# Hybrid decoder layer on one core: inputs of the dense products first on ACT and DVE, and a third buffer for their outputs

## The chip, the core and the metric

The kernel runs on one core of one Trainium2 chip. The metric is the device time of one execution in microseconds (us), as the median of several runs. A core has five engines with instruction queues of their own, each worked off in order: TensorE (PE, with its weight loads as PEld), VectorE (DVE), ScalarE (ACT), GpSimd (POOL) and SyncE (SP), which here issues all the DMAs.

## The reference

One layer on x (1024 x 1024, float32) with conditioning c. Cut to what matters:

```python
mod = c_act @ ada_w[l] + ada_b[l]
shift1, scale1, gate1, shift2, scale2, gate2 = [m[:, None, :] for m in jnp.split(mod, 6, axis=-1)]
h = x * (1.0 + scale1) + shift1
z = h @ w_in[l]                                   # 1024 x 3984
z_h, z_g, z_r = jnp.split(z, [N_HGRN_COLS, N_HGRN_COLS + N_GLA_COLS], axis=-1)
o_h = hgrn2_mixer(z_h, lower_bounds[l], hgrn_norm_g[l])
o_g = gla_mixer(z_g, gla_alpha_up[l], gla_alpha_b[l], gla_norm_g[l])
o_r = rwkv7_mixer(z_r, rwkv_mu[l], rwkv_w0[l], ...)
o = jnp.concatenate([o_h, o_g, o_r], axis=-1) @ w_out[l]
x = layer_norm(DEEPNORM_ALPHA * x + (1.0 + gate1) * o, ln1_g[l], ln1_b[l])
h = x * (1.0 + scale2) + shift2
m = jnp.square(jax.nn.relu(h @ mlp_w_up[l])) @ mlp_w_down[l]   # inner width 4096
x = layer_norm(DEEPNORM_ALPHA * x + (1.0 + gate2) * m, ln2_g[l], ln2_b[l])
```

The three mixers are recurrences over the sequence. All 16 heads carry a state from one chunk to the next, so the mixers of one piece of the sequence follow those of the piece before.

## The kernel before

The sequence is cut into two blocks of 512 positions, and each block into four tiles of 128 for the mixers. Three kinds of work stand in the program.

**Dense products.** The input projection (`z_block`, `z_rest`, `z_last`, here z(0) and z(1) for the two blocks), the output projection with its layer norm (`out_block`) and the MLP (`mlp_chunk`, `mlp_last`). They are computed in split single precision: each operand is a rounded part and a rest, and `mm3` (lines 1328 to 1330) runs three matmuls for each product. `split` makes the two parts: ACT rounds (`wh`, `ah`, line 1278) and DVE takes the rest (`wl`, `al`, line 1279; line 1276 with a scale). A slab of weights is 128 x 512, comes by DMA into a ring `raw` of 5 buffers, and has rings of 4 for `wh` and `wl`; moving operands have rings of 12, `ah` and `al`. Results lie in PSUM tiles `dn` (`tn` late in the program). They are taken out into a ring of 512-wide tiles tagged `s2`, which the profile shows as `s`: z goes out through them (ACT line 1373 or DVE line 1375; for the RWKV columns ACT line 1217 and DVE line 1218) and from there by DMA (lines 1377, 1379) to arrays in device memory, zr, zgc, zgt, zhc and zht; the relu of the MLP is there too (line 1499, then lines 1502 to 1504), and the modulated input of the MLP (`moving`, lines 1298 and 1300, after PE transposes in line 1293). `s2` has 2 buffers.

**Mixers.** `mixers` (line 336) runs over the tiles of a block as a software pipeline: signals, decays, attention by levels (`la_attn`, with DVE lines 417 to 423 and PE line 434), the triangular inverse of the RWKV part (`rw_base`, a DVE loop in lines 701 and 703 on tiles `btw` and `btm` of 48 partitions), and its chain (`rw_chain`). Their tiles come from pools of their own (`mp`, `psm`). They read z from device memory and write their outputs (lines 538 and 825) to an array oD, from which `out_block` reads (line 1305). mix(0) and mix(1) are the mixers of the two blocks, la_end (line 532) is the end of the attention part of a tile.

**Modulation.** `ada_first` and `ada_later` multiply and sum on DVE (line 1244), with weights in tiles `xt`.

**The order.** The class `Order` lays down, while the program is built, in which order each engine's instructions stand. It plays the program through with a cost for every instruction. Each instruction has a rank, made of a level (`level`, called in `build`) and its place in the program; an engine that is free takes the ready instruction of lowest rank whose tiles have room (`pick`, line 1059). mix(0) and mix(1)'s first tiles have level 0, z(1) has level 2, the MLP level 3 and more. So on ACT and DVE the mixers go ahead of z(1) and the MLP wherever both are ready. PE has a rule more: when few dense columns lie in the recent past (`behind`, line 1045), it takes a dense product first.

```python
            if e == PE and behind():
                for x in sorted(ready[e]):
                    if dense[x[1]] and fits(x[1]):
                        return take(x)
```

z(1) and mix(0) stand beside each other; then out_block(0), with z_last(1), the last part of z(1), beside its layer norm; then `mlp_moving`, and mix(1) beside the MLP of block 0, whose rest and the MLP of block 1 run alone.

Of the kernel before, what the change touches and what calls it, by code (L numbers as in the profile page):

```python
# [10 lines left out]
F32 = mybir.dt.float32  # L11
# [8 lines left out]
P = 128  # L20
# [99 lines left out]
class Kern:  # L120
# [83 lines left out]
    def setup_mixers(self, masks, wau, alpha_up, g_up, nrm):  # L204
# [7 lines left out]
        col = self.col  # L212
        self.wau = self.cp.tile([P, 384], F32, name="wau")
        self.load(self.wau, wau)
        self.aup = self.cp.tile([16, 384], F32, name="aup")
        self.load(self.aup, alpha_up)
        self.gup = self.cp.tile([P, 384], F32, name="gup")
        self.load(self.gup, g_up)
# [459 lines left out]
    def rw_base(self, s):  # L678
        nc = self.nc

        blk = self.dr.tile([4, 64, 3, 64], F32, tag="blk", bufs=2, name=self.nm("blk"))
        inv = self.inv[self.ninv % 2]
        self.ninv += 1
        step = 16 * 192 + 16
        for ca in range(4):
            c, a = divmod(ca, 2)
            nc.sync.dma_start(blk[ca], s["E"][c][64 * a:64 * a + 64, a, :, 0:64])
        TW = self.mt([48, 16, 2, 16], "btw")
        X, W = TW[:, :, 0, :], TW[:, :, 1, :]
        for g in range(12):  # L690
            ca, p = divmod(g, 3)
            src = blk[ca, :, p, :].rearrange("(m i) (n j) -> m i n j", i=16, j=16)
            nc.sync.dma_start(X[4 * g:4 * g + 4], self.diag(src))
        nc.vector.memset(W, 0.0)
        nc.vector.memset(TW.rearrange("p s x t -> p (s x t)")[:, 16:512:33], 1.0)
        tmp = self.mt([48, 64], "btm")
        eng = nc.vector
        for t in range(15, 0, -1):
            n = 16 - t
            tv = tmp[:, 0:t * n].rearrange("p (s j) -> p s j", j=n)  # L700
            eng.tensor_tensor(tv, X[:, 0:t, t:t + 1].broadcast_to([48, t, n]),
                              W[:, t:t + 1, t:16].broadcast_to([48, t, n]), ALU.mult)
            eng.tensor_tensor(W[:, 0:t, t:16], W[:, 0:t, t:16], tv, ALU.add)
        nc.scalar.copy(X, W.rearrange("p s t -> p t s"))
        for g in range(12):
            ca, p = divmod(g, 3)
            c, a = divmod(ca, 2)
            dst = inv[c, 64 * a:64 * a + 64, :, p, :].rearrange("(m i) x (n j) -> m (i x) n j", i=16, j=16)
            nc.sync.dma_start(self.diag(dst), TW[4 * g:4 * g + 4].rearrange("m i x j -> m (i x) j"))
        s["TW"] = self.mt([P, 2, 2, 3, 64], "TW")  # L710
        nc.sync.dma_start(s["TW"].rearrange("s c x p t -> s c (x p t)"), inv.rearrange("c s x p t -> s c (x p t)"))

# [127 lines left out]
F32_WEIGHT, T_WEIGHT = 1.3, 3  # L840

KEEP = 1.2

SWITCH, ISSUE = 130, 20
DMA_ISSUE, DMA_START, DMA_END = 500, 600, 900
# [28 lines left out]
class Order:  # L874
# [141 lines left out]
    def run(self):  # L1016
# [24 lines left out]
        recent, self.sum = collections.deque(), 0  # L1041
        dense = [self.eng[k] == PE and self.ins[k].ins[0].bass_ap.dtype == F32R for k in range(n)]


        def behind():
            while recent and recent[0][0] < t - HAM_TICK:
# [12 lines left out]
        def pick(e):  # L1059
            held = []  # L1060

            def take(x):
                ready[e].remove(x)
                heapq.heapify(ready[e])
                return x[1]

            if e == PE and run:
                x = self.rank[run[0]]
                if x not in ready[e]:
                    return None  # L1070
                run.pop(0)
                return take(x)
# [94 lines left out]
class Full(Kern):  # L1167
# [121 lines left out]
    def moving(self, parts, scale=None, shift=None, late=False, aside=False):  # L1289
        nc = self.nc  # L1290
        ps = self.tps() if late else self.dps()
        for j in range(TPB):
            nc.tensor.transpose(ps[:, j * P:(j + 1) * P], parts[j], self.ident)  # L1293
        if shift is None:
            return self.split(ps, "a", AB, late=late, scale=scale)
        h = self.dt([P, 512], "s2", 2)
        if aside:
            nc.scalar.activation(h, ps, AF.Identity, scale=scale, bias=shift)
        else:
            nc.vector.tensor_scalar(h, ps, scale, shift, ALU.mult, ALU.add)  # L1300
        return self.split(h, "a", AB, late=late)
# [7 lines left out]
    def x_moving(self, b, k, aside=False):  # L1309
        nc = self.nc  # L1310
        x = self.dt([P, 512], "raw", RB)
        h = x if b else self.dt([P, 512], "s2", 2)
        nc.sync.dma_start(x, self.A["xt"][k * P:(k + 1) * P, b * NT:(b + 1) * NT])
        scale, shift = self.mod[:, 8 + k:9 + k], self.mod[:, k:k + 1]
        if aside:
# [45 lines left out]
    def z_block(self, b):  # L1361
# [3 lines left out]

        def put(dst, rows, cols, n):
            def f(m, ps):
                t = self.dt([P, 512], "s2", 2)
                self.flip ^= 1
                if dst is self.zr[b]:  # L1370
                    self.shift(b, rows // P + m, t, ps)
# [93 lines left out]
    def out_block(self, b, late, lv=None):  # L1465
# [5 lines left out]
        for hf in range(2):  # L1471
            cs = slice(hf * 512, (hf + 1) * 512)
            gr = self.row(2, cs, late)

            def ev(t, ps):
                r = self.dt([P, 512], "raw", LR, late=True) if late else self.dt([P, 512], "s2", 2)
                nc.sync.dma_start(r, x[b * NT + t * P:b * NT + (t + 1) * P, cs])
                nc.vector.tensor_tensor(ys[t][:, cs], ps, gr, ALU.mult)
                nc.vector.scalar_tensor_tensor(ys[t][:, cs], r, ALPHA, ys[t][:, cs], ALU.mult, ALU.add)
            self.prod_t(self.A["w_out"][0][:, cs], o, ev, self.tps if late else None)  # L1480
# [12 lines left out]
    def mlp_up(self, fc, h, late):  # L1493
# [1 line left out]
        us = []  # L1495

        def evu(m, ps):
            r = self.dt([P, 512], "s2", 2)
            nc.scalar.activation(r, ps, AF.Relu)  # L1499
            hi = self.dt([P, 512], "ah", AB, F32R, late)  # L1500
            lo = self.dt([P, 512], "al", AB, F32R, late)
# [42 lines left out]
    def mlp_last(self, b, h, acc):  # L1544
# [13 lines left out]
                self.residual(b, acc, gate[:, cs], cs, t)  # L1558

        def add(t, hf, ps):  # L1560
            y = self.dt([P, 512], "s2", 2)
            cs = halves[hf]
            nc.vector.tensor_tensor(y, ps, gate[:, cs], ALU.mult)
            nc.vector.tensor_tensor(acc[t][:, cs], acc[t][:, cs], y, ALU.add)
# [116 lines left out]
```

## Time and profile before

| | before |
|---|---|
| median of 3 runs | 1505.16 us (1505.06 to 1505.33) |
| the profiled execution: its own time | 1511.53 us |
| the profiled execution: its span | 1509.7 us |
| PE busy | 1416.9 us, 94% of the span |
| PEld (weight loads) busy | 1131.9 us, 75% |
| DVE busy | 1052.7 us, 70% |
| ACT busy | 708.0 us, 47% |
| POOL busy | 25.4 us, 2% |
| mean granted clock of TensorE | 0.975 |

The span runs from the first to the last instruction. [...] "Waits" give the idle time of an engine ahead of an instruction and what ended it. Windows count us from the start of the span.

### The profile page before, as it was taken

To read this page: it belongs to the slowest core of one execution; us is meant where nothing else is said; L and a number is where in the kernel's file an instruction comes from. 1 tells how busy PE (TensorE), PEld (TensorE's weight loads), DVE (VectorE), ACT (ScalarE), POOL (GpSimd) and SP (SyncE) were. 2 spreads that over 40 slices of the span, in tenths; PEclk is the share of its full clock that TensorE was granted. 3 is DMA by queue.
4 is the path that set the end of the run, shared out by engine and by line. 5 is a ranking of instruction groups with operands and counts; after the bars stand their busy time and mean duration, and the time that the engine had idled before them with its cause. 6 is when DMAs were issued, how large, how long until landed. Compare 5 with 4: busy or idle time off the path is not lost.

```text
span 1509.7 us, 29223 instructions
## 1 busy us (share of the span) xinstructions
PE 1416.9 (94%) x11226; PEld 1131.9 (75%) x11226; DVE 1052.7 (70%) x2130; ACT 708.0 (47%) x1527; POOL 25.4 (2%) x32
## 2 busy tenths in 40 slices
PE   6999998889899896989899999999999999999996
PEld 5878876667787675767677788787887888888884
DVE  8787479889785576979788765475569445445478
ACT  3543365677756544666657443323343323333331
POOL 1000000000000000000000000000000000000004
PEclk9999999999989997999999999999999999999998
DMA  9998662524424655142423243454336432333331
GB/s 349 331 340 290 191 191 68 164 80 142 125 86 131 197 171 190 51 133 69 122 80 89 67 153 94 143 182 155 91 93 217 144 96 93 97 93 97 94 116 56
DMA packets 163291, 214.00 MB, mean 142 GB/s; under 512 B 39856, under 2 KB 90192, under 8 KB 163152
## 3 DMA queue, kind: packets, MB, share of 16 engines
q1 hardware_dynamic: 163152, 212.14, 44.6%
q8 instruction: 88, 1.44, 0.4%
q14 instruction: 51, 0.42, 0.1%
HBM read 180.03 MB, written 32.06 MB: 140 GB/s over the span
## 4 chain that ended last, share of the span: by engine, by line
PE 47%; DVE 7%; ACT 3%; DMA 2%; issue 1%; POOL 1%; SPq 0%; DVEq 0%; ACTq 0%; POOLq 0%
PE dn L1330 10%; PE dn L1328 10%; PE dn L1329 10%; PE tn L1330 5%; PE tn L1329 5%; PE tn L1328 5%; DMA lnr<-in_ln_b_dram 1%; DVE wl L1279 1%; DMA G<-zgt 1%; PE ml L434 0%; ACT L154 0%; DVE Rs L423 0%; DVE xt L1462 0%; DVE ld L459 0%; PE tn L1293 0%
## 5 line engine op out<-in xcount | busy, mean ns | idle before, releaser
L1278 ACT CAST wh<-raw 128x512 fp32r<-128x512 f32 (+2 forms) x424 | 253.0, 599 | 538.2 <-PE dn L1330 253.3
L1279 DVE TENSOR_TENSOR wl<-raw,wh 128x512 fp32r<-128x512 f32 (+2 forms) x424 | 278.3, 661 | 303.1 <-ACT wh L1278 279.5
L1328 PE MATMUL dn<-wh,ah 128*128 128x512 f32 (+1 forms) x736 | 288.3, 395 | 10.1 <-ACT s L1373 3.4
L1329 PE MATMUL dn<-wl,ah 128*128 128x512 f32 (+1 forms) x736 | 289.9, 394 | 4.6 <-DVE wl L1279 4.6
L1330 PE MATMUL dn<-wh,al 128*128 128x512 f32 (+1 forms) x736 | 287.8, 396 | 4.5 <-DVE al L1504 4.5
L1328 PE MATMUL dn<-ah,wh 128*128 128x512 f32 x560 | 226.7, 406 | 18.6 <-ACT ah L1321 11.4
L1329 PE MATMUL dn<-al,wh 128*128 128x512 f32 x560 | 225.8, 403 | 0.0
L1330 PE MATMUL dn<-ah,wl 128*128 128x512 f32 x560 | 223.5, 402 | 0.9 <-DVE wl L1279 0.7
L1328 PEld LDWEIGHTS dn<-wh,ah 128*128 128x128 f32 x736 | 141.6, 193 | 42.2 <-ACT s L1499 5.2
L1330 PEld LDWEIGHTS dn<-wh,al 128*128 128x128 f32 x736 | 141.6, 193 | 33.2 <-DVE al L1504 6.6
L1329 PEld LDWEIGHTS dn<-wl,ah 128*128 128x128 f32 x736 | 142.3, 193 | 31.3 <-DVE wl L1279 5.3
L1328 PEld LDWEIGHTS dn<-ah,wh 128*128 128x128 f32 x560 | 106.5, 190 | 45.2 <-ACT ah L1321 11.4
L1330 PEld LDWEIGHTS dn<-ah,wl 128*128 128x128 f32 x560 | 105.7, 189 | 24.4 <-DVE wl L1279 2.0
L1329 PEld LDWEIGHTS dn<-al,wh 128*128 128x128 f32 x560 | 106.3, 190 | 22.5 <-issue 0.9
L1330 PE MATMUL tn<-ah,wl 128*128 128x512 f32 x256 | 100.8, 394 | 0.0
L1329 PE MATMUL tn<-al,wh 128*128 128x512 f32 x256 | 100.2, 391 | 0.0
L1328 PE MATMUL tn<-ah,wh 128*128 128x512 f32 x256 | 99.6, 389 | 0.0
L157 ACT ACTIVATE ld<-ld 128x320 f32<-128x320 f32 (+1 forms) x120 | 54.8, 489 | 25.7 <-DVE ld L417 17.5
L1519 DVE TENSOR_TENSOR xt<-xt,dn 128x512 f32<-128x512 f32 x104 | 64.4, 679 | 0.1
L1244 DVE SCALAR_TENSOR_TENSOR xt<-xt,xt 128x1024 f32<-128x1024 f32 x48 | 58.3, 1216 | 8.3 <-DMA xt<-in_ada_wt_dram 8.0
L1329 PEld LDWEIGHTS tn<-al,wh 128*128 128x128 f32 x256 | 48.1, 188 | 11.2
L1328 PEld LDWEIGHTS tn<-ah,wh 128*128 128x128 f32 x256 | 48.1, 188 | 10.6
(288 smaller groups left out, 1960.5 us busy)
## 6 DMA issues: line engine op xcount, KB each, us to landing
raw<-in_mlp_w_up_dram SPq DMA_DIRECT2D x128, 256.0 KB
raw<-in_mlp_w_down_dram SPq DMA_DIRECT2D x128, 256.0 KB
xt<-in_ada_wt_dram SPq DMA_DIRECT2D x48, 512.0 KB
raw<-in_w_in_dram SPq DMA_DIRECT2D x64, 256.0 KB
raw<-in_w_in_dram SPq DMA_DIRECT2D x48, 192.0 KB
raw<-in_w_out_dram SPq DMA_DIRECT2D x32, 256.0 KB
raw<-in_w_in_dram SPq DMA_DIRECT2D x32, 196.0 KB
raw<-in_xt_dram SPq DMA_DIRECT2D x24, 256.0 KB
```

Source lines behind the costliest of these rows:

```text
L157: ins = nc.scalar.activation(out, in_, func, **kw)
L1244: nc.vector.scalar_tensor_tensor(w, w, 1.0, self.cact, ALU.mult, ALU.mult, accum_out=self.sums[:, q:q + 1])
L1278: nc.scalar.copy(hi[:, 0:n], src)
L1279: (eng or nc.vector).tensor_tensor(lo[:, 0:n], src, hi[:, 0:n].bitcast(F32), ALU.subtract)
L1328: nc.tensor.matmul(ps, lh, rh, start=first, stop=False)
L1329: nc.tensor.matmul(ps, lh, rl, start=False, stop=False)
L1330: nc.tensor.matmul(ps, ll, rh, start=False, stop=last)
L1519: nc.vector.tensor_tensor(acc[t][:, cs], acc[t][:, cs], ps, ALU.add)
```

## The change

Three edits. `Order.pick` gets a rule for ACT and DVE: an instruction that uses a tile of the dense products' pools (`dp`, `psd`, `tp`, `pst`) is taken ahead of any other that is ready, whatever its rank, if its tiles have room. The ring `s2` has 3 buffers in place of 2, at each of its uses. And the RWKV inverse's tile `btw` (48 partitions) no longer comes from the mixers' pool: it shares one array `ab` with the small weight `aup` (16 partitions), `btw` at partitions 64 to 111 and `aup` at 0 to 15; `btm` moves to partitions 64 to 111 too.

```diff
--- before.py
+++ after.py
@@ -212,7 +212,9 @@
         col = self.col
         self.wau = self.cp.tile([P, 384], F32, name="wau")
         self.load(self.wau, wau)
-        self.aup = self.cp.tile([16, 384], F32, name="aup")
+
+        self.ab = self.cp.tile([P, 512], F32, name="ab")
+        self.aup = self.ab[0:16, 0:384]
         self.load(self.aup, alpha_up)
         self.gup = self.cp.tile([P, 384], F32, name="gup")
         self.load(self.gup, g_up)
@@ -685,7 +687,7 @@
         for ca in range(4):
             c, a = divmod(ca, 2)
             nc.sync.dma_start(blk[ca], s["E"][c][64 * a:64 * a + 64, a, :, 0:64])
-        TW = self.mt([48, 16, 2, 16], "btw")
+        TW = self.ab[64:112].rearrange("p (i x j) -> p i x j", i=16, x=2)
         X, W = TW[:, :, 0, :], TW[:, :, 1, :]
         for g in range(12):
             ca, p = divmod(g, 3)
@@ -693,7 +695,7 @@
             nc.sync.dma_start(X[4 * g:4 * g + 4], self.diag(src))
         nc.vector.memset(W, 0.0)
         nc.vector.memset(TW.rearrange("p s x t -> p (s x t)")[:, 16:512:33], 1.0)
-        tmp = self.mt([48, 64], "btm")
+        tmp = self.mt([P, 64], "btm")[64:112]
         eng = nc.vector
         for t in range(15, 0, -1):
             n = 16 - t
@@ -841,6 +843,8 @@
 
 KEEP = 1.2
 
+DENSE = ("dp", "psd", "tp", "pst")
+
 SWITCH, ISSUE = 130, 20
 DMA_ISSUE, DMA_START, DMA_END = 500, 600, 900
 
@@ -1041,6 +1045,9 @@
         recent, self.sum = collections.deque(), 0
         dense = [self.eng[k] == PE and self.ins[k].ins[0].bass_ap.dtype == F32R for k in range(n)]
 
+        feeds = [self.eng[k] in (ACT, DVE) and any(t.split("_")[-2] in DENSE for t, _ in self.uses[k])
+                 for k in range(n)]
+
 
         def behind():
             while recent and recent[0][0] < t - HAM_TICK:
@@ -1064,6 +1071,10 @@
                 heapq.heapify(ready[e])
                 return x[1]
 
+            if e in (ACT, DVE):
+                for x in sorted(ready[e]):
+                    if feeds[x[1]] and fits(x[1]):
+                        return take(x)
             if e == PE and run:
                 x = self.rank[run[0]]
                 if x not in ready[e]:
@@ -1293,7 +1304,7 @@
             nc.tensor.transpose(ps[:, j * P:(j + 1) * P], parts[j], self.ident)
         if shift is None:
             return self.split(ps, "a", AB, late=late, scale=scale)
-        h = self.dt([P, 512], "s2", 2)
+        h = self.dt([P, 512], "s2", 3)
         if aside:
             nc.scalar.activation(h, ps, AF.Identity, scale=scale, bias=shift)
         else:
@@ -1309,7 +1320,7 @@
     def x_moving(self, b, k, aside=False):
         nc = self.nc
         x = self.dt([P, 512], "raw", RB)
-        h = x if b else self.dt([P, 512], "s2", 2)
+        h = x if b else self.dt([P, 512], "s2", 3)
         nc.sync.dma_start(x, self.A["xt"][k * P:(k + 1) * P, b * NT:(b + 1) * NT])
         scale, shift = self.mod[:, 8 + k:9 + k], self.mod[:, k:k + 1]
         if aside:
@@ -1365,7 +1376,7 @@
 
         def put(dst, rows, cols, n):
             def f(m, ps):
-                t = self.dt([P, 512], "s2", 2)
+                t = self.dt([P, 512], "s2", 3)
                 self.flip ^= 1
                 if dst is self.zr[b]:
                     self.shift(b, rows // P + m, t, ps)
@@ -1473,7 +1484,7 @@
             gr = self.row(2, cs, late)
 
             def ev(t, ps):
-                r = self.dt([P, 512], "raw", LR, late=True) if late else self.dt([P, 512], "s2", 2)
+                r = self.dt([P, 512], "raw", LR, late=True) if late else self.dt([P, 512], "s2", 3)
                 nc.sync.dma_start(r, x[b * NT + t * P:b * NT + (t + 1) * P, cs])
                 nc.vector.tensor_tensor(ys[t][:, cs], ps, gr, ALU.mult)
                 nc.vector.scalar_tensor_tensor(ys[t][:, cs], r, ALPHA, ys[t][:, cs], ALU.mult, ALU.add)
@@ -1495,7 +1506,7 @@
         us = []
 
         def evu(m, ps):
-            r = self.dt([P, 512], "s2", 2)
+            r = self.dt([P, 512], "s2", 3)
             nc.scalar.activation(r, ps, AF.Relu)
             hi = self.dt([P, 512], "ah", AB, F32R, late)
             lo = self.dt([P, 512], "al", AB, F32R, late)
@@ -1558,7 +1569,7 @@
                 self.residual(b, acc, gate[:, cs], cs, t)
 
         def add(t, hf, ps):
-            y = self.dt([P, 512], "s2", 2)
+            y = self.dt([P, 512], "s2", 3)
             cs = halves[hf]
             nc.vector.tensor_tensor(y, ps, gate[:, cs], ALU.mult)
             nc.vector.tensor_tensor(acc[t][:, cs], acc[t][:, cs], y, ALU.add)
```

In the changed file the lines of the mixers have numbers 2 higher, and those of the dense products 11 higher. The set of instructions is the same; all that moves is their order, up to some 2800 of the 5168 dense matmuls and transposes, and a few at the program's very end.

DVE at the second tile of mix(0), where the RWKV inverse and the attention levels meet (`wl` is a dense weight slab's rest; `TW`, `btw`, `ab`, `btm` belong to the inverse, `ld` and `b` to the attention). Before:

```order
L1279 TENSOR_TENSOR wl_5339<-raw_5336,wh_5338 128x384
L739 COPY_PREDICATED TW_2094<-masks,mr_2864 32x2x3x16 x2
L743 COPY TW_2094<-mr_2864 16x2x3x16 x2
L417 TENSOR_TENSOR ld_3174<-b_2702 128x640
L417 TENSOR_TENSOR ld_3203<-b_2702 128x640
L758 COPY TW_2094<-mr_2934 32x2x3x32
L694 MEMSET btw_2802 48x16x16
L758 COPY TW_2094<-mr_2934 32x2x3x32
L695 MEMSET btw_2802 48x16
L701 TENSOR_TENSOR btm_2817<-btw_2802 48x15
L703 TENSOR_TENSOR btw_2802<-btw_2802,btm_2817 48x15
```

With the change, from the same place:

```order
L1290 TENSOR_TENSOR wl_5443<-raw_5440,wh_5442 128x384
L741 COPY_PREDICATED TW_2092<-masks,mr_2861 32x2x3x16 x2
L745 COPY TW_2092<-mr_2861 16x2x3x16 x2
L419 TENSOR_TENSOR ld_3171<-b_2700 128x640
L419 TENSOR_TENSOR ld_3200<-b_2700 128x640
L760 COPY TW_2092<-mr_2931 32x2x3x32 x2
L696 MEMSET ab 48x16x16
L423 TENSOR_TENSOR ld_3171<-ld_3171,K_2676 128x20x16
L1290 TENSOR_TENSOR wl_5458<-raw_5455,wh_5457 128x384
```

Before, the `wl` at the head is the last for 30 rows; now the next comes after eight.

PE where mix(0) ends and out_block(0) begins (`dn<-consts,raw` is the transposes of oD, `dn<-ah,wh` and its like are products of z(1), `mr` and `ml` belong to mixers). Before:

```order
L1328 MATMUL dn_5951<-ah_5018,wh_6082 128x512
L1293 MATMUL dn_6112<-consts,raw_6110 128x128 x4
L1329 MATMUL dn_5951<-al_5019,wh_6082 128x512
L1330 MATMUL dn_5951<-ah_5018,wl_6083 128x512
L1328 MATMUL dn_5952<-ah_5018,wh_6082 128x512
L1329 MATMUL dn_5952<-al_5019,wh_6082 128x512
L1330 MATMUL dn_5952<-ah_5018,wl_6083 128x512
L1328 MATMUL dn_5953<-ah_5018,wh_6082 128x512
L1329 MATMUL dn_5953<-al_5019,wh_6082 128x512
L1330 MATMUL dn_5953<-ah_5018,wl_6083 128x512
L1293 MATMUL dn_6123<-consts,raw_6121 128x128 x4
```

With the change:

```order
L1341 MATMUL dn_5949<-ah_5014,wl_6079 128x512
L499 MATMUL ml_4705<-V_4177,ld_4689 64x64 x10
L1275 MATMUL ml_4747<-consts,mod 8x128
L1275 MATMUL ml_4827<-consts,mod 8x128
L390 MATMUL ml_7175<-consts,al_7140 16x128
L296 MATMUL mr_6901<-zm_6884,wau 128x128
L298 MATMUL mr_6900<-wk_6895,wau 128x128
L296 MATMUL mr_6901<-zm_6884,wau 128x128
L298 MATMUL mr_6900<-wk_6895,wau 128x128
L296 MATMUL mr_6901<-zm_6884,wau 128x128
L298 MATMUL mr_6900<-wk_6895,wau 128x128
L1304 MATMUL dn_6108<-consts,raw_6106 128x128 x4
```

Before, products of z(1) stand up to and among the transposes, and the last state update of mix(0) (line 497) has 124 of them behind it; now that update (line 499) and mixer work of mix(1) alone stand between the last product of z(1) and the transposes.

ACT at the end of z_last(1), ahead of the MLP's modulated input (line 1373 takes results out to `s`, line 1298 makes the input). Before:

```order
L1373 COPY s_1252_6788<-dn_6584 128x512
L1373 COPY s_1253_6791<-dn_6585 128x512
L1278 CAST wh_10030<-raw_10028 128x512
L1373 COPY s_1254_6794<-dn_6586 128x512
L1373 COPY s_1255_6797<-dn_6587 128x512
L1298 ACTIVATE s_1261_6816<-dn_6811,mod 128x512
L1278 CAST ah_6807<-s_1257_6805 128x512
```

With the change:

```order
L1384 COPY s_1248_6784<-dn_6580 128x512
L1384 COPY s_1249_6787<-dn_6581 128x512
L1384 COPY s_1250_6790<-dn_6582 128x512
L1289 CAST wh_10022<-raw_10020 128x512
L1384 COPY s_1251_6793<-dn_6583 128x512
L621 COPY bs_7060<-mr_7047 128x6
L1309 ACTIVATE s_1257_6812<-dn_6807,mod 128x512
L1289 CAST ah_6803<-s_1253_6801 128x512
```

Before, two results are taken out before a cast of weights and two behind it; now three stand in a row, and mixer work (`bs`) stands between the fourth and the input.

## Rows read from the trace of the kernel before

**Rows 1.** The query on the core: span, and mean granted clock of TensorE.

```profile
core 0: 1509.7 us, clock 0.975
```

**Rows 2.** Windows by stage: us, busy (instructions) by engine, PE clock, DMA share, GB/s.

```profile
100.00:150.00 50.00, 45.93 (x290) 40.70 (x289) 39.47 (x99) 21.33 (x55) 0.00 (x0) 0.93 0.90 292
150.00:210.00 60.00, 58.67 (x268) 48.47 (x267) 33.01 (x64) 23.13 (x44) 0.00 (x0) 1.00 0.63 196
210.00:497.00 287.00, 266.25 (x3691) 206.59 (x3689) 229.15 (x558) 189.99 (x484) 0.00 (x0) 0.96 0.39 117
497.00:605.00 108.00, 90.27 (x381) 71.39 (x380) 69.47 (x132) 51.19 (x93) 1.86 (x2) 0.88 0.60 190
605.00:890.00 285.00, 266.15 (x3588) 204.22 (x3588) 238.68 (x541) 177.80 (x435) 0.00 (x0) 0.98 0.29 85
890.00:950.00 60.00, 60.00 (x265) 49.23 (x264) 29.61 (x48) 18.96 (x32) 0.00 (x0) 1.00 0.47 143
950.00:1470.00 520.00, 516.16 (x2267) 419.46 (x2266) 302.78 (x484) 171.53 (x285) 3.44 (x4) 1.00 0.40 123
```

**Rows 3.** Waits of PE in 210:497: us in total, times, longest.

```profile
PE dn L1328 <- DVE s L1218: 4.5, 4, 2.5
...
PE dn L1328 <- ACT s L1373: 1.4, 1, 1.4
```

**Rows 4.** Waits of PE in 605:890.

```profile
PE dn L1328 <- ACT s L1499: 2.1, 2, 1.3
...
PE dn L1330 <- DVE al L1504: 1.7, 3, 1.3
...
PE dn L1328 <- DVE xt L1517: 1.0, 1, 1.0
```

**Rows 5.** Waits of PE in 100:210.

```profile
PE dn L1328 <- ACT s L1373: 3.4, 2, 1.9
PE dn L1328 <- DVE s L1375: 1.1, 1, 1.1
```

**Rows 6.** Timeline at the second seam: start us, us, engine, line, operation, [idle before <-releaser].

```profile
585.27 1.40 SPq L1377 DMA_DIRECT2D zht<-s  x2
...
588.23 1.22 ACT L1373 COPY s<-dn 128x512 f32<-128x512 f32 x2 [0.50 <-DMA zht<-s]
...
588.87 0.42 SPq L318 DMA_DIRECT2D V<-zht  x1
...
590.76 0.49 SPq L327 DMA_DIRECT2D G<-zht  x1
...
594.10 0.81 DVE L1300 TENSOR_SCALAR s<-dn,mod 128x512 f32<-128x512 f32 x1 [5.64 <-DMA G<-zht]
...
594.65 0.78 ACT L1298 ACTIVATE s<-dn,mod 128x512 f32<-128x512 f32 x1 [5.20 <-DMA zht<-s]
...
594.96 1.97 PE L1293 MATMUL dn<-consts,xt 128*128 128x128 f32 x8 [4.79 <-DVE s L1300]
```

**Rows 7.** Line 538 in 400:520: count, duration, start of the first and the last.

```profile
L538 SPq DMA_DIRECT2D oD<-o x2: 319/322/326, 415.2 to 463.8; - x2
```

**Rows 8.** Timeline at the first seam.

```profile
497.48 0.60 PE L1293 MATMUL dn<-consts,raw 128*128 128x128 f32 x4
...
508.11 1.65 PE L1328 MATMUL dn<-wh,ah 128*128 128x512 f32 x3 [1.40 <-ACT wh L1278]
```

**Rows 9.** Windows of 10 us with a lower clock, columns as in rows 2.

```profile
390.00:400.00 10.00, 7.04 (x43) 5.88 (x42) 7.01 (x16) 9.52 (x24) 0.00 (x0) 1.00 0.58 163
400.00:410.00 10.00, 7.80 (x97) 6.70 (x98) 4.62 (x11) 8.06 (x23) 0.00 (x0) 0.89 0.72 215
410.00:420.00 10.00, 10.00 (x121) 8.27 (x120) 6.22 (x14) 4.12 (x10) 0.00 (x0) 0.50 0.30 90
420.00:430.00 10.00, 10.00 (x121) 8.53 (x119) 7.31 (x16) 6.35 (x17) 0.00 (x0) 0.76 0.16 42
```

**Rows 10.** The dearest group of DVE: count | busy us, mean ns | idle before.

```profile
L1279 DVE TENSOR_TENSOR wl<-raw,wh 128x512 fp32r<-128x512 f32 x344 | 235.3, 687 | 287.4 <-ACT wh L1278 263.9 <-PE tn L1329 12.3 <-PE dn L1329 8.1
```

## The prediction

> **What bounds the kernel now.** I read the span first, then the windows by stage, then PE's waits in each stage, and last single stretches of the timeline. The span is 1509.7 us at a mean clock of 0.975 [rows 1]; the profiled execution took 1511.53 us by its own time, 6.4 us above the median of the runs, 1505.16. The sum below is made against 1511.53 and carried over to the median by taking off 6.4.
>
> The windows show where PE is the limit and where it isn't [rows 2]. From 950 to 1470 us PE is busy for 516.2 of 520 us at the full clock: the MLP without mixers leaves nothing to gain. From 890 to 950 it is busy all the time, with 265 matmuls in 60 us, or 0.226 us each. The losses lie earlier, where mixers run. In 210:497 (mix(0) beside z(1)) PE is idle for 287 - 266.25 = 20.8 us, and the clock of 0.96 costs 287 x 0.04 = 11.5. In 605:890 (mix(1) beside the MLP) it is idle for 18.9, and the clock of 0.98 costs 5.7. In 497:605 (output projection, layer norm, start of the MLP) it is idle for 17.7, and 0.88 costs 13.0. In 100:210 it is idle for 4.1 + 1.3 = 5.4, and 0.93 over 50 us costs 3.5. That makes 62.8 of idle time and 33.7 of clock: 96.5 us is all that a better order could give back.
>
> DVE is not the limit as a mean (229 of 287, 239 of 285 us), but it comes in bursts: before the change 30 DVE rows in a row belong to mixers, while PE's stock of slabs runs out.
>
> **The change, part by part.** The instructions are the same, so no engine's work grows; a `wl` costs 687 ns wherever it stands [rows 10]. The shared array costs nothing: the inverse's rows have as many elements per partition as before, and the loads and stores are the same; `aup` is only read after its load. It could cost one wait, of an inverse's loads on the stores of the one before, and that wait was there with the one `btw` buffer already. What pays or costs is the order.
>
> *Mix(0) beside z(1).* PE's waits for dense inputs and for PSUM that a dense result still holds are 4.5 + 1.4 = 5.9 us [rows 3]. They are waits on just the ACT and DVE work that now goes first; I take them whole. The other 20.8 - 5.9 = 14.9 us are mostly waits on mixer steps. Those steps themselves get later, but a stock of slabs lets the order put products in front of them: bounds 0 and 14.9, and I take a quarter, 3.7, nearer to 0 because the PE order keeps most of these waits one behind another. The clock: 410:420 stands at 0.50 and 420:430 at 0.76, right behind two windows in which PE is busy for 7.04 and 7.80 of 10 us [rows 9]. With less idle time some of it goes; of 11.5 I take a third, 3.8. Sum: -13.4.
>
> *Mix(1) beside the MLP.* The same, by its rows [rows 4]: 2.1 + 1.7 + 1.0 = 4.8 whole, a quarter of the other 14.1 (3.5), a third of the clock's 5.7 (1.9). Sum: -10.2. mix(1) now ends some 210 dense products later; behind it lie about 2,440 of them at 0.226 us, so nothing waits for it.
>
> *100:210.* The waits for results to be taken out are 3.4 + 1.1 us [rows 5]. The third `s2` buffer and the rule both bear on them; I take half, -2.
>
> *Second seam, the start of the MLP.* The store of the first results of z_last(1) is issued at 585.27, the last two results are taken out by 588.23 + 1.22 = 589.45, and both `s2` buffers then wait for their stores: the first inputs of the MLP are made at 594.10 and 594.65, and PE stands for 4.79 us until then [rows 6]. With three buffers the first input can take the one whose store had already let line 1373 go on at 588.23. So the 4.65 us between 589.45 and 594.10 go, bounds 0 (if the store then in flight is what counts) and 4.79. Fewer idle us, and mixer products of mix(1) that now stand here, should also lift the clock: a quarter of 13.0. Sum: -8.
>
> *First seam, mix(0) to out_block(0).* Here the change costs. The last oD store of mix(0)'s attention is issued at 463.8 [rows 7], and the transposes that read it start at 497.48 [rows 8]: 33.7 us of cover, filled with 124 products of z(1). Since dense work ran ahead, that cover is spent: behind the last state update only mixer products of mix(1) remain. PE must now wait for la_end, the store and the load. From the second seam: store issue to the dependent load's issue is 588.87 - 585.27 = 3.6 us, and a load issued at 590.76 has its user running at 594.10, 3.3 us [rows 6], together 6.9; the tail of la_end ahead of it and the mixer products that fill part of it about cancel, and I add 1.1 for the first slab of w_out behind it: 508.11 still waits 1.40 us for one [rows 8]. So +8. Bounds: 0, and the whole 33.7.
>
> A lower clock behind this wait would be a second price: 410:430 lost 5.0 + 2.4 = 7.4 us that way [rows 9]. I leave it out of the sum, since 497:605 already has a clock of 0.88 that I only lift by a quarter. [...]
>
> *The end.* POOL's scalar for the third tile of the last block now goes ahead of its wide multiplies, and DVE finishes that tile before the fourth. What one gains the other waits for: 0, within 2 either way.
>
> Sum: -13.4 - 10.2 - 2 - 8 + 8 = -25.6. 1511.5 - 25.6 = 1485.9 on the profiled execution's scale, 1479.5 on that of the median: **1480 us**. With the first seam at 15 and the mixer stages at half their terms it is 1498, with that seam at 0 and the mixer stages at half as much again 1460.
>
> **The rivals.**
>
> *A larger gain.* A busy PE is not a PE at its peak. In 890:950 the weight loads are busy for 49.23 of 60 us, 82%; in 210:497 for 206.6 of 287, in 605:890 for 204.2 of 285, both 72% [rows 2]. So the mixer stages hide slack in busy time. If products there came in longer runs and the share rose half-way, to 77%, the stages would take 268 and 265 us, 38.5 less in place of my 23.6: 1465. Against it: in the new order PE changes between dense and mixer products 432 times, before 406. [...]
>
> *The seams give it back.* If nothing fills the first seam, it costs up to 33.7 in place of 8, and the total comes to 1505: no change. For it: the whole chain of the last tile now ends together with z(1). Against it: parts of that chain still have products beside them.
>
> *Slower: mixers late.* Engines work in order, and PE's order is fixed. If on the chip DVE's mixer steps come later than the order allows for, because each stands behind a `wl` of 0.69 us, PE stands in front of mixer products with dense ones ready behind them. Each such case costs 0.69; the gain of 25.6 is eaten at 37 cases, or one in twelve of the 432 changes. At one in eight, 54 cases, 37 us: 1517, slower. For it: some 70% of PE's idle time in 210:497 is for mixers already. Against it: DVE has 58 us free there [rows 2].
>
> *The third buffer does nothing.* If the MLP's input waits at the second seam for stores anyway, the 4.65 us stay: 1484.
>
> **How the numbers follow.** My sum 52%, the third buffer idle 6%, a larger gain 17%, seams give it back 12%, mixers late 13%. A difference of 0.2%, 3 us, is about what measurements can tell from none. The first three are faster (75), of the seams I count 3 as faster, 5 as same and 4 as slower, and mixers late is slower: faster 0.78, same 0.05, slower 0.17. The likeliest case alone spans 1460 to 1498. The range goes down to 1452 for most of the larger gain, and up to 1512 for the seams and part of the late mixers; about 2 in 10 stay out, on both sides.
>
> **What would show it.** Right: PE's idle time in the two mixer stages falls by a third to a half, waits of dense products on lines 1218, 1499 and 1504 (11 numbers higher there) nearly go, the 4.79 us at the MLP's start shrink, and a wait of some 8 us or more stands new ahead of the transposes of out_block(0). Wrong: waits of PE on mixer steps longer in sum than today's 29 us over both stages, a clock below 0.975, or a first seam beyond 20 us.

## The result: 0.7% faster, and the profile after

| | before | after |
|---|---|---|
| median | 1506.57 us (6 runs, 1505.06 to 1512.50) | 1497.57 us (6 runs, 1490.46 to 1500.45) |
| ratio | | 0.9929, 95% interval 0.9911 to 0.9947 |
| profiled execution | 1511.53 us, span 1509.7, clock 0.975 | 1494.09 us, span 1492.3, clock 0.985 |

The change gains 9 us; 25.6 were forecast. 1497.57 lies inside the range of 1452 to 1512, but over 17 us above the number. The two profiles are 17.4 us apart because that of before stands 5 us above its median and that of after 3.5 below: half of what they show is no property of the kernels.

The page of after, its first part (busy us, share of the span, instructions):

```profile
span 1492.3 us, 29276 instructions
...
PE 1404.9 (94%) x11226; PEld 1122.7 (75%) x11226; DVE 1081.4 (72%) x2130; ACT 704.3 (47%) x1527; POOL 24.1 (2%) x32
```

The windows of after by stage, with the columns of [rows 2]. The cuts at 481 and 592 lie where its dense products stand at the same place as at 497 and 605 before; the last row goes on to 918, where `mix(1)` now ends:

```profile
100.00:150.00 50.00, 45.77 (x291) 40.51 (x290) 40.28 (x93) 21.39 (x54) 0.00 (x0) 0.93 0.90 306
150.00:210.00 60.00, 57.67 (x260) 48.30 (x259) 34.67 (x73) 22.39 (x41) 0.00 (x0) 0.97 0.59 177
210.00:481.00 271.00, 255.48 (x3565) 199.39 (x3564) 227.32 (x518) 173.46 (x435) 0.00 (x0) 0.99 0.40 117
481.00:592.00 111.00, 92.61 (x505) 73.55 (x504) 74.83 (x132) 58.65 (x112) 1.87 (x2) 0.92 0.64 199
592.00:918.00 326.00, 311.55 (x3804) 238.89 (x3803) 285.06 (x620) 203.32 (x493) 0.00 (x0) 0.99 0.33 94
```

PE is idle for 15.5 us in the third row, 14.5 in the fifth; [rows 2] had 20.8 and 18.9. What it waits for in after, over the whole span (the first row stands at the program's start, and was 11.4 before):

```profile
PE dn L1339 <- ACT ah L1332: 11.7, 1, 11.7
PE dn L1304 <- DMA raw<-oD: 8.0, 1, 8.0
PE dn L1339 <- ACT s L1384: 4.5, 3, 3.2
PE ml L436 <- DVE Rs L425: 4.5, 10, 0.6
PE mr L642 <- DVE bon L628: 4.1, 5, 1.1
PE dn L1341 <- DVE al L1515: 3.0, 2, 1.5
```

The new wait ahead of the transposes of `oD` is there, 8.0 us long. Sorted by who waits, the waits of dense products in the two mixer stages fall from 12.1 us to 4.4 (all rows of the views behind [rows 3, 4], summed), as the rule should bring; those of mixer products go from 26.1 to 24.0 only. So the gain that is missing is missing in the mixers' own chain.

To compare kernels whose stages end at different times I count PE's idle time in each trace (gaps between one matmul and the next) up to the k-th of the 5,168 dense matmuls. k = 750 is where `mix(0)` has begun, 1488 the end of z(1), 1530 behind the first seam, 1840 the start of the MLP, 2800 a place behind all mixers. The last column is the mended kernel, `fix`, of the fourth group below.

| idle us of PE, dense products | before | after | forecast of the difference | mended |
|---|---|---|---|---|
| up to 750 | 15.7 | 18.8 | -2 | 18.2 |
| 750 to 1488, `mix(0)` | 22.1 | 16.6 | -9.6 | 9.1 |
| 1488 to 1530, first seam | 4.2 | 13.8 | +8 | 13.1 |
| 1530 to 1840, second seam | 13.5 | 4.5 | -4.7 | 5.4 |
| 1840 to 2800, `mix(1)` | 18.9 | 14.5 | -8.3 | 6.9 |
| sum | 74.4 | 68.2 | -16.6 | 52.7 |

### The profile page after: what moved, and what is told of

Its sections match the earlier page's. It is cut to its first block, busy times and chain, and to the rows that moved or that the text cites. A ratio compares the mean times of both kernels' runs of the same rounds, so it can differ in the third digit from the quotient of the medians.

```text
span 1492.3 us, 29276 instructions
## 1 busy us (share of the span) xinstructions
PE 1404.9 (94%) x11226; PEld 1122.7 (75%) x11226; DVE 1081.4 (72%) x2130; ACT 704.3 (47%) x1527; POOL 24.1 (2%) x32
## 4 chain that ended last, share of the span: by engine, by line
PE 43%; DVE 10%; ACT 4%; issue 2%; DMA 1%; SPq 1%; POOL 1%; DVEq 0%; ACTq 0%; POOLq 0%
PE dn L1341 9%; PE dn L1340 9%; PE dn L1339 9%; PE tn L1341 5%; PE tn L1340 5%; PE tn L1339 5%; DVE wl L1290 1%; DVE Rs L425 1%; ACT wh L1289 1%; DVE btm L703 1%; DVE ab L705 1%; DVE ld L419 1%; DVE xt L1473 0%; DVE ld L423 0%; ACT L154 0%
## 5 line engine op out<-in xcount | busy, mean ns | idle before, releaser
L1341 PE MATMUL dn<-wh,al 128*128 128x512 f32 (+1 forms) x736 | 284.1, 390 | 3.0 <-DVE al L1515 3.0
```

Source lines behind the costliest of these rows:

```text
L1341: nc.tensor.matmul(ps, ll, rh, start=False, stop=last)
```

## The experiments

Every time is a median, every ratio is to runs of the kernel before on the same chip, with its 95% interval.

### One part of the change at a time

`buf3` drops the rule (the first lines below) and keeps the shared array and three buffers; `rule2` keeps rule and shared array with two buffers; in `first` the rule acts on instructions ahead of `out_block(0)` alone (the last lines), in `second` on those from there on.

```diff
-            if e in (ACT, DVE):
-                for x in sorted(ready[e]):
-                    if feeds[x[1]] and fits(x[1]):
...
-        h = self.dt([P, 512], "s2", 3)
+        h = self.dt([P, 512], "s2", 2)
...
-                 for k in range(n)]
+                 and k < self.seam for k in range(n)]
```

> The shared array and the third s2 buffer, without the rule for ACT and DVE. Theory A (the rule makes most of the gain, the buffer only mends the start of the MLP): 5 us less than before, 0.997, the 4.8 us wait of PE at the MLP's start gone, the mixer stages as before. Rival B (the buffer makes the gain, since results that wait for a buffer hold PSUM): 10 us less or more, 0.993, and waits of PE on lines 1217 to 1220 and 1373 gone in mix(0). Rival C (nothing in particular makes it, any new order differs by as much): anything from -10 to +10.

> The rule for ACT and DVE with two s2 buffers. Theory A: 5 us less than before, 0.997, with the long wait ahead of the transposes of oD as in the change (some 15 us idle in the seam) and the wait at the MLP's start back. Rival B: as before or slower, 1.000 to 1.005, since the rule alone has only the seam to show.

> Three buffers, the rule only for instructions that the program has ahead of out_block(0), so for z(1) beside mix(0). Theory A': what the first stage gains (some 6 us) is lost again at the first seam, where the transposes of oD wait: 1 to 8 us slower than with the buffer alone. Theory A as forecast: both stages pay by themselves, so some 5 us faster than the buffer alone.

> Three buffers, the rule only for instructions from out_block(0) on. Theory A': the best of the four, 12 to 16 us less than before (0.990 to 0.992), with the first seam as before (13 us from the last product of z(1) to the thirtieth of out_block(0), not 26) and the second stage as in the change. Rival C: no clear order among the four.

Measured: `buf3` 1537.16 (1.0217, 1.0198 to 1.0236), `rule2` 1511.03 (1.0041, 1.0028 to 1.0053), `first` 1525.97 (1.0137, 1.0119 to 1.0155), `second` 1523.78 (1.0109, 1.0088 to 1.0129). Only `rule2` came out as one of the theories had it (rival B, 1.000 to 1.005); theory A of `first` has the direction (5 us faster than the buffer alone; it is 11), and no theory has `buf3` or `second`. Each part by itself is slower than before, and only both together are faster. Without the rule the kernel is 31 us slower than before. In each stage the rule takes that loss away for that stage: with `first` z(1) ends at 478 us, as in after (483), with `second` at 530, as in `buf3` (525). But `first` loses most of it again: its 42 products at the first seam take 27 us for 9 in `buf3`, and the mixers beside the MLP, where the rule doesn't act, 376 us for 359 (from the 1,840th dense product to the 2,800th).

### Is any new order a draw?

One cost of the plan changed a little, in the kernel before, in `buf3` and in the change:

```diff
-SWITCH, ISSUE = 130, 20
+SWITCH, ISSUE = 140, 20
```

> The kernel before, with one cost of the plan changed a little (SWITCH 130 to 140): two output buffers, no rule, only another ready-made order. Theory D: what counts is how many dense products stand beside each tile of mixers; in this order 110, 155 and 115 stand between the last state updates of mix(0)'s tiles, 380 in all, against 415 before and 373 in the run with three buffers and no rule, so this kernel should lose most of what that one lost: 1520 to 1535. Theory B: the third buffer itself is at fault (outputs leave in bursts); with two buffers nothing is lost: 1500 to 1512.

> Three output buffers, no rule, SWITCH 140: between the last state updates of mix(0) stand 112, 118 and 124 dense products, 354 in all, fewer than in the run with SWITCH 130 (373). Theory D: as slow as that run or slower, 1535 to 1550. Theory B: the same as that run, 1537 within 5. Theory C (any order is a draw, whatever the buffers and the rule): anything from 1500 to 1540.

> The change, with SWITCH 140 in place of 130: rule and three buffers, another order (154, 200 and 123 dense products between the last state updates of mix(0), 477 in all; the change has 481). Theories D and B: 1497 within 6. Theory C: as far off as the other draws, 20 us or more.

Measured: 1506.01 (1.0001, 0.9986 to 1.0015), 1540.65 (1.0215, 1.0189 to 1.0241), 1497.56 (0.9938, 0.9916 to 0.9960). Three other orders (PE changes between dense and mixer products 26 times more often, 18 times less and 16 times more than in the orders they come from), the same three times: theory C, that any order is a draw, falls as far as these three orders go. So does theory D, that the count of dense products beside a tile decides: 380 in `n_before` cost nothing.

### The rule on one engine, and a filled seam

`dve` and `act` apply the rule on one engine (`if e == DVE:`, `if e == ACT:`). `tail2` exempts `mix(0)`'s last steps (`self.late`, a range of instructions) from being passed over:

```diff
         feeds = [self.eng[k] in (ACT, DVE) and any(t.split("_")[-2] in DENSE for t, _ in self.uses[k])
-                 for k in range(n)]
+                 or self.late[0] <= k < self.late[1] for k in range(n)]
```

> Three buffers, the rule on DVE alone; ACT takes its work by rank. 159, 214 and 96 dense products stand between the last state updates of mix(0), 1488 lie ahead of the last one (the change: 166, 194, 121 and 1488). Theory T: a tile of mixers takes 66 to 77 us in every run, and only the dense products beside it count: as the change, 1494 to 1503. Theory of ACT (its table loads and casts are what PE waits for): 1515 or more.

> Three buffers, the rule on ACT alone. 115, 151 and 134 dense products stand between the last state updates of mix(0), 1334 ahead of the last one (three buffers without the rule: 131, 112, 130 and 1307). Theory T: 27 more products beside mixers at 0.226 us in mix(0), about as many as without the rule in mix(1): 1528 to 1535. Theory of ACT: 1500 or less.

> The change, but from the second step of mix(0)'s pipeline on its own ACT and DVE work is not passed over, so that 89 products of z(1) remain behind its last state update and cover the way of oD through memory. The first seam's 13 us of idle time should go. Theory D: the products that cover the seam are missing beside the tiles (123, 131, 132 in place of 166, 194, 121), and that stage loses 10 to 25 us again: 1497 to 1515. Theory A' (the seam is what eats the gain): 1480 to 1488.

Measured: `dve` 1509.16 (1.0018, 1.0004 to 1.0032), `act` 1524.65 (1.0125, 1.0104 to 1.0147), `tail2` 1500.89 (0.9961, 0.9944 to 0.9977). Against `buf3` DVE's half of the rule is worth 28 us and ACT's 12.5, together about the whole 39.6; both times lie outside what either theory had. In `tail2` the first seam takes 12.8 us for its 42 products where the change takes 26.1; but z(1) ends 17.5 us later, and the sum is 3 us worse. That is within theory D's 1497 to 1515, though `n_before` spoke against its count.

### Orders kept, the arrays and the buffer alone

`p2` has three buffers on the chip, no rule, and a plan that is told of two; every engine's order is then that of the kernel before, row for row. `p2r` is the same with the rule, in the order of `rule2`.

```diff
-                    self.room[t.tag] = t.tag_meta.bufs
+                    self.room[t.tag] = 2 if t.tag.startswith("s2_") else t.tag_meta.bufs
```

> Three output buffers on the chip, no rule, but the plan is told that there are two: every engine's order is that of the kernel before. Theory O: the 31 us that the third buffer costs without the rule sit in the order that the plan writes with it, not in the buffer: 1506 or up to 8 us less, if the waits for stores at the MLP's start (4.7 us) go. Theory B: a third buffer on the chip itself hurts (outputs leave in bursts): 1520 to 1540.

> As the run before, with the rule: the order of the run with the rule and two buffers (1511.0), on a chip that has three. Theory O: the buffer alone is worth little, 1505 to 1511, and most of the 13 us between the rule with two buffers and the change come from another order. Theory S: the buffer frees the waits for stores at the seams: 1497 or less.

Measured: `p2` 1526.31 (1.0149, 1.0125 to 1.0172), `p2r` 1508.20 (1.0015, 1.0000 to 1.0030). The second says that the buffer as such does little, in an order not made for it. The first is the surprise: 20 us slower with no instruction in another place. Its number is that of theory B, but the buffer isn't the reason, as `part64` below shows: it has two buffers and is no faster. Laid beside each other row by row, the DVE rows of `p2` and of before run apart at the 30 steps of each tile's inverse of 16 x 16 blocks, which the shared array has moved from partitions 0 to 47 to 64 to 111. That gave the next four.

`part64` is the kernel before with that move alone, two arrays, two buffers, no rule:

```diff
-        TW = self.mt([48, 16, 2, 16], "btw")
+        TW = self.mt([P, 16, 2, 16], "btw")[64:112]
...
-        tmp = self.mt([48, 64], "btm")
+        tmp = self.mt([P, 64], "btm")[64:112]
```

`fix` is the change with the two residents of the shared array exchanged; `fix_buf3` is `buf3` with the same exchange; `rule_apart` is the kernel before with the rule alone.

```diff
-        self.aup = self.ab[0:16, 0:384]
+        self.aup = self.ab[64:80, 0:384]
...
-        ha = self.wl()[0:16, 0, :]
+        ha = self.wl()[64:80, 0, :]
...
-        TW = self.ab[64:112].rearrange("p (i x j) -> p i x j", i=16, x=2)
+        TW = self.ab[0:48].rearrange("p (i x j) -> p i x j", i=16, x=2)
...
-        tmp = self.mt([P, 64], "btm")[64:112]
+        tmp = self.mt([P, 64], "btm")[0:48]
```

> The kernel before, its order unchanged, two buffers, no rule, the two small arrays apart as before: only the array of the 16 x 16 inverses and its scratch stand on partitions 64 to 111 in place of 0 to 47. Theory P: a DVE row that starts on partition 64 next to rows that start on 0 loses the overlap that two neighbours otherwise have (0.105 us for each pair in the run with before's order, 3.6 us from the first to the last step of one tile): 1520 to 1530. Theory S (it is the sharing of one array that costs, by waits on it): 1506 within 4.

> The change, order and all, but the inverses stand on partitions 0 to 47 of the shared array and the other array on 64 to 79. Theory P: about 4 us less for each tile whose steps are on the path, six or seven of eight: 1470 to 1483. Theory S: 1497 within 5. If P holds, the forecast of 1480 lacked this term alone.

> Three buffers without the rule (1537), the inverses on partitions 0 to 47: same order as that run. Theory P: 20 to 30 us less, 1507 to 1517, so that the third buffer's order itself costs at most 10. Theory S: 1537 within 5.

> The kernel before with the rule alone: two buffers, the two arrays apart, the order of the run with rule, shared array and two buffers (1511.0). Theory P: 18 to 28 us less than that run, 1483 to 1493. Theory S: 1505 to 1511.

Measured: `part64` 1530.35 (1.0154, 1.0127 to 1.0181), `fix` 1469.64 (0.9747, 0.9717 to 0.9777), `fix_buf3` 1519.51 (1.0077, 1.0048 to 1.0105), `rule_apart` 1487.62 (0.9870, 0.9841 to 0.9899). All four go the way of theory P and none that of theory S, though only `rule_apart` lies inside P's range (`part64` is 0.4 us above it, `fix` 0.4 below, `fix_buf3` 2.5 above). The place of the inverses costs 24 us by itself, 18 in the order of `buf3`, 23 in that of `rule2` and 28 in the change, whose order `fix` keeps on every engine. `fix` still shares the array, so the sharing isn't the cause. `rule_apart` also sets the first group right: the rule by itself was slower than before only because the inverses had moved; without the move it is 1.3% faster. `fix` beats both before and after, and is 2.5% faster than before.

DVE's timeline at the same piece of `mix(0)`'s second tile, in before (start, duration, engine, line, operation):

```profile
240.34 0.81 DVE L417 TENSOR_TENSOR ld<-b 128x640 f32<-128x640 f32 x1
241.07 0.17 DVE L703 TENSOR_TENSOR btw<-btw,btm 48x28 f32<-48x28 f32 x1
241.17 0.81 DVE L417 TENSOR_TENSOR ld<-b 128x640 f32<-128x640 f32 x1
241.91 0.18 DVE L701 TENSOR_TENSOR btm<-btw 48x39 f32<-48x39 f32 x1
242.02 0.48 DVE L421 TENSOR_TENSOR ld<-ld,K 128x320 f32<-128x320 f32 x1
242.42 0.19 DVE L703 TENSOR_TENSOR btw<-btw,btm 48x39 f32<-48x39 f32 x1
242.64 0.36 DVE L783 COPY UV<-mr 64x192 f32<-64x192 f32 x1
```

and in `part64`:

```profile
244.97 0.83 DVE L417 TENSOR_TENSOR ld<-b 128x640 f32<-128x640 f32 x1
245.83 0.19 DVE L703 TENSOR_TENSOR btw<-btw,btm 48x28 f32<-48x28 f32 x1
246.05 0.83 DVE L417 TENSOR_TENSOR ld<-b 128x640 f32<-128x640 f32 x1
246.90 0.20 DVE L701 TENSOR_TENSOR btm<-btw 48x39 f32<-48x39 f32 x1
247.13 0.49 DVE L421 TENSOR_TENSOR ld<-ld,K 128x320 f32<-128x320 f32 x1
247.65 0.20 DVE L703 TENSOR_TENSOR btw<-btw,btm 48x39 f32<-48x39 f32 x1
247.77 0.36 DVE L783 COPY UV<-mr 64x192 f32<-64x192 f32 x1
```

In before the row at 241.07 starts ahead of the end of the one before it (240.34 + 0.81 = 241.15), and the next, at 241.17, ahead of 241.24. In `part64` 244.97 + 0.83 = 245.80 is followed at 245.83, and 246.02 at 246.05: a gap of 0.03 where there was an overlap of 0.07. The last row turns it round: this `UV` works on partitions 64 to 127, and now it overlaps its neighbour on 64 (247.65 + 0.20 against 247.77), while in before it waits behind the one on 0 (242.42 + 0.19 against 242.64). So it isn't that partition 64 is slow; what is lost is the overlap of neighbours of which one starts on 0 and the other on 64. Over the whole trace such a step has a neighbour in 455 places: in before 310 of them overlap and the gaps sum to -20.8 us, in `part64` 38 overlap and they sum to +10.0 (waits over 0.1 us left out). Where the neighbour writes all 128 partitions, and so starts on partition 0, 276 of 309 overlap in before and none of 325 in `part64`. That is 31 us in eight tiles, on an engine that mixers wait for. The steps' own time is the smaller part, 2.3 us. The rest of the work on the moved array doesn't explain the loss: ACT's copy of it (line 704) takes 5.2 us in both kernels, and DVE waits 5.6 us for its loads in before, 5.8 in `part64`. The steps' groups in before (count | busy us, mean ns | idle before):

```profile
L703 DVE TENSOR_TENSOR btw<-btw,btm 48x15 f32<-48x15 f32 (+7 forms) x120 | 23.3, 194 | 0.8
L701 DVE TENSOR_TENSOR btm<-btw 48x15 f32<-48x15 f32 (+7 forms) x120 | 23.1, 193 | 1.1
```

and in `part64`:

```profile
L703 DVE TENSOR_TENSOR btw<-btw,btm 48x15 f32<-48x15 f32 (+7 forms) x120 | 24.4, 203 | 3.4
L701 DVE TENSOR_TENSOR btm<-btw 48x15 f32<-48x15 f32 (+7 forms) x120 | 24.3, 203 | 3.2
```

The lost overlap is some 0.105 us for each neighbour, 0.075 of overlap and 0.031 of gap (medians). Only starts at 0 and 64 were run, so what other pairs of starts cost was not shown.

What the mend is worth in the stages, by the windows of `fix`:

```profile
210.00:466.00 256.00, 248.27 (x3552) 196.23 (x3551) 214.16 (x515) 171.89 (x433) 0.00 (x0) 0.99 0.41 120
466.00:578.00 112.00, 93.43 (x503) 74.41 (x503) 74.23 (x131) 58.37 (x112) 1.87 (x2) 0.91 0.65 197
578.00:894.00 316.00, 309.22 (x3805) 239.32 (x3804) 273.05 (x621) 203.83 (x493) 0.00 (x0) 0.99 0.34 97
```

DVE is busy for 13 us less in the first and 12 less in the last than the same work takes in after, 25 together, and the two stages are 25 us shorter. The waits of mixer products, 24.0 us in after, come to 9.1.

### The first seam once more, in the mended kernel

`fix_tail2` is `fix` with the edit of `tail2`.

> The mended change (inverses on partitions 0 to 47), and from the second step of mix(0)'s pipeline on its own ACT and DVE work is not passed over, so 89 products of z(1) remain behind its last state update and cover the way of oD through memory. Theory A' (the first seam's 25 us for 42 products, 13.5 before, is lost gain): 1458 to 1464. Theory D (the products that cover the seam are then missing beside mix(0)'s tiles): 1468 to 1476, as the same edit without the mend came out 3 us above the change.

Measured: 1475.12 (0.9787, 0.9763 to 0.9811), 5.5 us above `fix` and within theory D's range. The seam takes 14.0 us in place of 25.3. `mix(0)`'s last state update comes 7.2 us earlier (461.0 us for 468.2), but z(1) ends 20.9 us later. PE's idle time only moves: at the seam it falls from 13.1 to 3.3 us, beside `mix(0)` it rises from 9.1 to 19.5. So products that cover the seam are worth no more there than beside the tiles.

## Why the forecast was wrong

*The failed step* is one sentence: "The shared array costs nothing: the inverse's rows have as many elements per partition as before, and the loads and stores are the same". Elements, loads and stores were compared, the start partition wasn't, though the diff shows it (`self.ab[64:112]`). It costs 28 us in the change, `fix` against after, 0.9747 against 0.9929. The trace of before could have told it: there, too, the copies on partitions 64 to 127 stand apart from the steps beside them (242.42 + 0.19 against 242.64 above; 24 such neighbours in the trace, none nearer than 0.030 us), where rows that start on partition 0 overlap them (276 of 309 above). With that term the sum of -25.6 would have been about +2, so the other terms were too small by some 11 us; without the term the forecast of 1480 stands 10 us above `fix`. The expectation of `fix` had this term as the only one missing; it is the main error, not the only one.

*Mix(0) beside z(1), -13.4, and mix(1) beside the MLP, -10.2.* The waits of dense work fell by 7.7 us, from 12.1 to 4.4, for the 10.7 that I took. Of the other waits I took a quarter. In the change they lose 2 of 26 us, since each tile's chain got longer; with the inverses on partition 0 they lose 17, two thirds. Idle time fell by 5.5 and 4.4 us in the change, by 13.0 and 12.0 in the mended kernel, for 9.6 and 8.3 forecast. The mechanism was right, and the forecast size lies between the two.

*The clock.* I took 5.7 us of clock in these stages and a quarter of 13.0 at the seam from [rows 2]. In the traces of before and of after the granted clock stands at 1.00 or at 0.50 alone, so a figure in between is a mean over its stretch. The profile of before lost 32.4 us to the clock by the 2,800th dense product (half of the time at 0.50), that of `n_before` 22.2, with the same idle time (74.4 and 74.5) and the same median. In the 77 executions of the kernel before that were timed beside the experiments the mean clock was 0.975 to 0.985, with a median of 0.981, so that the profiled one, at 0.975, is at the low end: 0.006 of 1510 is 9 us. Some ten us of what I took for a property of the kernel belonged to that one execution. The six executions of the change have a median of 0.985; 0.004 of 1500 is 6 us of clock gained, for the 9 that I had summed.

*100:210, -2.* Wrong in sign: up to the 750th dense product there are 3.1 us more of idle time, 1.2 of them in these two windows. In `fix` it is 2.5, so it isn't the inverses; the cause stays open.

*Second seam, -8.* Idle time fell by 9.0. The third buffer was only part of the reason. With before's order and three buffers (`p2`) this stretch is idle for 12.6 us, where it was 13.5; with an order made for three buffers and no rule (`buf3`) for 8.3, with the rule and two (`rule2`) for 7.8, with both for 4.5. The rival "the third buffer does nothing" held in the two kernels whose order was not made for it, `p2` and `p2r` (7.9).

*First seam, +8.* Idle time rose by 9.6, 8.0 of it the wait that the chain of store and load was to bring; 42 products take 26.1 us in place of 13.5, so +12.6. Most of the rest is mixer products, the last state update of `mix(0)` and then work of `mix(1)`: with them and two small transposes of the modulation PE is busy for 3.2 us between the last product of z(1) and the wait (483.69 to 489.65), and before has none of them in this seam. The clock is the smaller part, since it is low in both kernels: in this seam PE is busy at 0.50 for 5.5 us in after and for 4.6 in before. There the 128x512 products of before start 0.43 us apart (509.55 to 512.97), at 1.00 0.23 us (514.21 to 514.90); by these paces, some 2.6 us lost in after for 2.1 in before, an estimate. Windows of after with the columns of [rows 2], then rows of PE's timeline:

```profile
480.00:490.00 10.00, 6.91 (x57) 4.93 (x55) 3.41 (x6) 8.38 (x23) 0.00 (x0) 0.94 0.54 181
490.00:500.00 10.00, 2.36 (x11) 2.02 (x12) 3.51 (x10) 4.69 (x11) 0.00 (x0) 0.50 0.94 248
```

```profile
488.32 0.37 PE L298 MATMUL mr<-wk,wau 64*128 64x128 f32 x1 [1.38 <-ACT wk L157]
...
489.02 0.63 PE L298 MATMUL mr<-wk,wau 64*128 64x128 f32 x2
497.64 4.59 PE L1304 MATMUL dn<-consts,raw 128*128 128x128 f32 x20 [7.99 <-DMA raw<-oD]
```

Against +8 that is an error of 4.6 us: 1.6 of idle time, and the rest mostly those mixer products. The 15 that the slower case of the sum takes for this seam is about 8 and the 7.4 us of [rows 9], an estimate that no run shows; +12.6 was measured. The transposes behind the wait start at a clock of 0.50. But 0.94 in 480:490 leaves some 1.2 us at 0.50 there, and in windows of 0.1 us the clock is 1.00 in 488.6:488.7 and 0.50 in 488.8:488.9: it had fallen ahead of the 8.0 us wait, which begins at 489.65. PE stood before that in shorter gaps between mixer products, the last of them 1.4 us. So the long wait can't be the cause of the fall; what caused it was not shown.

*The end, 0.* From the 2,800th to the 5,150th dense product: 539.8 us before, 538.9 after.

*The rivals.* "Mixers late" named the right place and the wrong reason: mixers did come later than the order allows, not behind a `wl` but behind their own inverse. "The seams give it back" is, in part, what the rule does with two buffers: in `rule_apart` z(1) ends at 462 us, earlier than in `fix`, and the stretch from there to the MLP takes 126.9 us against 106.5. That is what the buffer is for: with the rule and an order made for it, it is worth 18 us (1487.62 to 1469.64).

Left open: why the order that the plan makes for three buffers without the rule is 13 us slower than before (`fix_buf3`).

## What to carry to other kernels

When an array is moved to share room, compare the start partition as well as the size, and look which engine works on it next to what: here the steps of a chain, 0.193 us each, lost some 0.105 us at a neighbour. Cut a change into its parts even where one of them looks like bookkeeping; here the smallest edit took away three quarters of the gain of the rest. And read a loss to the clock from more than one execution before a term is built on it.

## What was not expected of the hardware

A step of the inverse and a DVE row beside it that writes all 128 partitions overlap by 0.075 us in before (the median), where both start on partition 0, and stand 0.031 us apart in after, where the step starts on 64: some 0.105 us a pair, more than half of the 0.193 us that such a step takes. The same kernel's order, moved by one cost, gave the same time within 0.3%, while the profiled executions of two kernels with equal idle time and equal medians, before and `n_before`, differ by 10 us in what they lost to the clock (32.4 and 22.2).
